# A fused FNet/retention layer with SwiGLU on one core: the seven products of each gate and up set in four parts by token group, in a new order

## The chip, the cores and the metric

The kernel runs on one core of one Trainium2 chip. The metric is device time in microseconds (us), from runs of the whole program; the profile is of one execution of the same program. TensorE is the matmul engine, VectorE, ScalarE and GpSimd work on rows in on-chip memory, and SyncE issues most transfers. In the profile they are PE, DVE, ACT, POOL and SP; PEld is TensorE's load of its stationary operand.

## The reference, cut to what matters

The layer mixes tokens (Fourier and retention heads), normalises, and then runs a SwiGLU on 2048 tokens of width 1024 with 2816 hidden columns. The change lies in the SwiGLU and in the norms just ahead of it:

```python
def swiglu(u, wg, wu, wd):
    return (jax.nn.silu(u @ wg) * (u @ wu)) @ wd
...
        x = layer_norm(DEEPNORM_ALPHA * x + gt1 * mix, ln1_g[l], ln1_b[l])
        u2 = modulate(layer_norm(x), sh2, sc2)
        x = layer_norm(DEEPNORM_ALPHA * x + gt2 * swiglu(u2, w_ffn_gate[l], w_ffn_up[l], w_ffn_down[l]),
                       ln2_g[l], ln2_b[l])
```

All inputs are f32. The kernel keeps f32 accuracy with f16 operands by splitting each number into a high and a low half.

## The kernel before, in words

**Products.** `u2 @ wg` and `u2 @ wu` are computed as 2x2 block products in the form of Strassen and Winograd: seven products in place of eight. Their names are A11, A12, A22 (blocks of the tokens' matrix) and S1 to S4 (sums and differences of such blocks, made by `left`). `right` makes the seven weight operands of one set, with subtracts on GpSimd and a split of each into halves (`split`: high half on ScalarE, L148, low half on VectorE, L149). One product is four steps over k of three matmuls each (`mm3`: high by high, high by low, low by high; L152 to L154), so twelve matmuls of 128x128 by 128x512.

**Sets.** The hidden columns are cut into 11 tiles (`j`), each with a gate set and an up set; a set is seven products for each of two token groups (`sb` 0 and 1). The operands of group 0 are the tiles u2b0 to u2b6 (read back from DRAM; in the order, the digit is the product: 0 A11, 1 A12, 2 S2, 3 S3, 4 A22, 5 S1, 6 S4), those of group 1 are u2a0 to u2a6 (written in place by the last norms).

**Banks.** Products that share a sum accumulate onto one PSUM bank. Bank x (proj for group 0, misc for group 1) takes A11, then S2, S3 and A22; between them ScalarE copies what stands in it (L1323): p after A11, a after S2, b after S3. The next product on x waits for the copy. Bank z (s0 and s1, in the profile both "s") takes S1, from which the fourth quadrant is b + z, and then S4, from which the second is a + z. Bank tq or zt takes A12. VectorE does the sums (L1310 for gate, L1317 for up), ScalarE the silu (L1311, L1308). `keep` copies, `done` sums, `product` ties both to a product. The first gate set is different: five of its products for group 0 run ahead of the last norms' transposes (`late()`), each in a bank of its own, and `alone` takes them up later.

**What sets the order.** Each engine runs its instructions in the order of the program, which a scheduler has interleaved by their dependencies and the order of the code. ORDER gives the seven products' sequence, and `right` makes the operands in that sequence. Weight operands live in a ring of 12 tiles (`ws_tile`, eight taken per set), raw weights in a ring of three (`raw_tile`). `down(i, c)` prepares the down weights beside the sets and stores them in DRAM; `down_last()` does this for the last tile, ahead of the last gate set. `u2_part` transposes and modulates the normalised rows xh (L1060) into q (L1071 to L1078), makes the seven operands and splits them (low halves in L1085).

Of the kernel before, what the change touches and what calls it, by code (L numbers as in the profile page):

```python
# [9 lines left out]
F32 = mybir.dt.float32  # L10
F16 = mybir.dt.float16
AF = mybir.ActivationFunctionType
ALU = mybir.AluOpType
PSUM = bass.MemoryType.PSUM

P = 128
# [63 lines left out]
def layer_kernel(ctx: ExitStack, tc: tile.TileContext, a, out):  # L80
# [50 lines left out]
    def ws_tile(shape=(P, 2, 512), dt=F16):  # L131
        return mk(wp, list(shape), dt, tag="ws", bufs=12)
# [828 lines left out]
    ORDER = (A11, A12, S2, S1, S3, A22, S4)  # L961
# [10 lines left out]
    def right(qa, qb):  # L972

        q0, q1, q2, q3 = qa[:, 0], qa[:, 1], qb[:, 0], qb[:, 1]
        ops = []

        def op(src):
            w = ws_tile()
            split(w[:, 0], w[:, 1], src)
            ops.append(w)  # L980

        t1 = ws_tile((P, 512), F32)
        op(q0)
        op(q2)
        G.tensor_tensor(q0, q1, q0, ALU.subtract)
        G.tensor_tensor(t1, q3, q0, ALU.subtract)
        G.tensor_tensor(q1, q3, q1, ALU.subtract)
        G.tensor_tensor(q2, q2, t1, ALU.subtract)

        for src in (t1, q0, q1, q2, q3):  # L990
            op(src)
        return [ops[ORDER.index(o)] for o in range(7)]

# [30 lines left out]
    def out_proj(t, between=None, last=False):  # L1024
# [12 lines left out]
        if last:  # L1037

            es_z.close()
            ub = es_l.enter_context(tc.tile_pool(name="u2b", bufs=1, reuse_waits="tile"))  # L1040
            for o in range(2, 7):
                u2_early(o, ub)
# [20 lines left out]
    def u2_part(sb, i, xh):  # L1063
# [18 lines left out]
        for o, src in enumerate(ops):  # L1082
            dst = u2[1][o][:, i] if sb else us[:, o]
            S.copy(dst[:, :, 0], src)
            (V if o in (2, 5) or (sb and i == 3 and o != 4) else G).tensor_tensor(dst[:, :, 1], src, dst[:, :, 0], ALU.subtract)  # L1085
# [23 lines left out]
    FIRST = 5  # L1109
    TAGS = ("proj", "misc", "proj", "misc", "s0")  # L1110
    TLAST = ("tq", "zt", "s1")
    late = None
    for sb in (0, 1):
        for i in range(4):
            if sb and i == 1:
                es_u.close()
                ue = es_l.enter_context(tc.tile_pool(name="u2e", bufs=1, reuse_waits="tile"))
                u2_early(0, ue)
                u2_early(1, ue)
# [16 lines left out]
    first = {(o, 0): prod(w0, o, 0, (TAGS[o],)) for o in range(FIRST)}  # L1136
    late()
    es_b.close()
# [111 lines left out]
    for j in range(HJ):  # L1250
# [37 lines left out]
        if j == HJ - 1:  # L1288
            down_last()
        for gu, src in enumerate((wg_in, wu_in)):  # L1290
# [8 lines left out]
            else:  # L1299
                w = w_ops(w_raws(src, j))  # L1300
            st = [{}, {}]
# [31 lines left out]
            def alone(o, sb, ps):  # L1333

                d = st[sb]
                if o == A11:
                    keep(sb, "p", ps)
                elif o == A12:
                    done(sb, 0, d["p"], ps)
                elif o == S2:  # L1340
                    d["a"] = mk(cq, [P, 512], tag="a", bufs=2)
                    V.tensor_tensor(d["a"], d["p"], ps, ALU.add)
                elif o == S3:
                    d["b"] = mk(cq, [P, 512], tag="b", bufs=2)
                    V.tensor_tensor(d["b"], d["a"], ps, ALU.add)
                elif o == A22:
                    done(sb, 2, d["b"], ps)
                elif o == S1:
                    V.tensor_tensor(d["a"], d["a"], ps, ALU.add)
                    done(sb, 3, d["b"], ps)  # L1350
                else:
                    done(sb, 1, d["a"], ps)

# [23 lines left out]
            if j == 0 and gu == 0:  # L1377
                for o in range(7):
                    alone(o, 0, first[o, 0] if (o, 0) in first else prod(w, o, 0, ALL_BANKS))
# [14 lines left out]
            else:  # L1394
                for o in ORDER:
                    for sb in range(2):
                        product(o, sb)
# [274 lines left out]
```

## Time and profile before

| | |
|---|---|
| median of 3 runs | 2142.61 us (2142.06 to 2146.86) |
| profiled execution | 2139.36 us |
| its span | 2137.5 us |
| mean granted clock of TensorE | 0.981 |
| busy: TensorE | 2029.4 us (95%) |
| busy: VectorE | 1404.2 us (66%) |
| busy: ScalarE | 792.0 us (37%) |
| busy: GpSimd | 764.3 us (36%) |

The span goes from the first to the last instruction of the profiled execution; 1.86 us of its time lie around it. The gate and up sets run from about 904 to 1750 us. "Busy" of TensorE counts a matmul until its modelled end. In rows of a timeline the numbers are the start and the duration in us; what stands in brackets is the idle time before the instruction and the instruction (engine, tile, line) that ended it.

### The profile page before, as it was taken

The numbers are of one execution on the slowest core, as the hardware profiler recorded it, in microseconds if no ns is written. First come the engines' busy times: TensorE is split into PE (matmuls) and PEld (weight loads), VectorE is DVE, ScalarE is ACT, GpSimd is POOL, SyncE is SP. The second block draws the span as 40 slices with busy tenths as digits, with TensorE's granted clock in tenths as the row PEclk, the third lists the DMA queues.
The fourth block names the chain that finished last, engine by engine and source line by source line (L and its number), as shares of the span: only waits on it lengthen the run. The fifth ranks groups of instructions, "written<-read, shape, count | busy, mean of one in ns | idle before, by whom it ended". The sixth has DMA issues, their size and how long they took to land. (4 is left out here: it accounts for less than half of the span.)

```text
span 2137.5 us, 30994 instructions
## 1 busy us (share of the span) xinstructions
PE 2029.4 (95%) x11678; PEld 1180.2 (55%) x11678; DVE 1404.2 (66%) x2545; ACT 792.0 (37%) x1436; POOL 764.3 (36%) x804
## 2 busy tenths in 40 slices
PE   6899989999999899979999999999999889999998
PEld 4456576468558444434444444444444348888743
DVE  7976384766547577786566556656664557878776
ACT  5625432242233244443433343334333324333132
POOL 3323312221222156556575557556755300000010
PEclk8999999999999999989999999999999999999999
DMA  9631122331311555634544444444444269665652
GB/s 289 189 107 55 33 64 69 115 95 50 92 37 60 168 169 200 231 119 123 161 126 134 126 144 125 140 122 142 131 144 150 71 224 333 215 220 205 244 183 104
DMA packets 300342, 305.19 MB, mean 143 GB/s; under 512 B 15448, under 2 KB 248992, under 8 KB 299040
## 3 DMA queue, kind: packets, MB, share of 16 engines
q1 hardware_dynamic: 293376, 287.08, 42.1%
q10 hardware_dynamic: 6816, 16.12, 2.0%
q8 instruction: 92, 1.51, 0.3%
q14 instruction: 58, 0.48, 0.1%
HBM read 200.25 MB, written 102.90 MB: 142 GB/s over the span
## 5 line engine op out<-in xcount | busy, mean ns | idle before, releaser
L152 PE MATMUL proj<-ws,uhi 128*128 128x512 f16 (+1 forms) x768 | 251.1, 327 | 4.4 <-ACT sg L774 3.2
L154 PE MATMUL proj<-ws,ulo 128*128 128x512 f16 (+1 forms) x768 | 251.2, 327 | 0.0
L153 PE MATMUL proj<-ws,uhi 128*128 128x512 f16 (+1 forms) x768 | 251.0, 327 | 0.0
L153 PEld LDWEIGHTS <-ws 128*128 128x128 f16 x1296 | 128.0, 99 | 173.2 <-issue 22.5
L152 PEld LDWEIGHTS <-ws 128*128 128x128 f16 x1296 | 127.9, 99 | 155.9 <-issue 7.6
L154 PEld LDWEIGHTS <-ws 128*128 128x128 f16 x1296 | 127.6, 98 | 155.4 <-issue 5.9
L167 POOL TENSOR_TENSOR rstd<-ve,mhalf 128x1 f32<-128x1 f32 x66 | 38.2, 589 | 451.3 <-DVE ve L165 438.1
L149 DVE SCALAR_TENSOR_TENSOR ws<-raw,ws 128x512 f16<-128x512 f32 x186 | 147.9, 810 | 63.4 <-ACT ws L148 62.3
L148 ACT ACTIVATE ws<-raw 128x512 f16<-128x512 f32 x186 | 112.5, 624 | 96.9 <-DMA raw<-in_w_ffn_gate_dram 25.3
L1157 ACT CAST ho<-h 128x1280 f16<-128x1280 f32 x70 | 87.4, 1258 | 148.4 <-DVE h L1429 37.2
L152 PE MATMUL proj<-u2b,ws 128*128 128x512 f16 x344 | 129.6, 381 | 10.8 <-ACT b L1323 8.7
L152 PE MATMUL misc<-u2a,ws 128*128 128x512 f16 x344 | 131.1, 381 | 4.7 <-ACT b L1323 3.9
L149 DVE SCALAR_TENSOR_TENSOR wdo<-raw,wdo 128x256 f16<-128x256 f32 (+1 forms) x100 | 67.6, 700 | 101.5 <-ACT wdo L148 99.6
L153 PE MATMUL proj<-u2b,ws 128*128 128x512 f16 x344 | 131.1, 381 | 0.0
L154 PE MATMUL misc<-u2a,ws 128*128 128x512 f16 x344 | 131.1, 381 | 0.0
L153 PE MATMUL misc<-u2a,ws 128*128 128x512 f16 x344 | 130.9, 381 | 0.0
L154 PE MATMUL proj<-u2b,ws 128*128 128x512 f16 x344 | 130.8, 381 | 0.0
L1158 DVE TENSOR_TENSOR ho<-h,ho 128x1280 f16<-128x1280 f32 x70 | 103.8, 1486 | 21.4 <-ACT ho L1157 21.3
L153 PEld LDWEIGHTS <-uhi 128*128 128x128 f16 x768 | 75.6, 98 | 47.1 <-issue 5.5
L154 PEld LDWEIGHTS <-ulo 128*128 128x128 f16 x768 | 75.6, 98 | 44.8
L152 PEld LDWEIGHTS <-uhi 128*128 128x128 f16 x768 | 76.0, 99 | 42.9 <-issue 1.3
L149 DVE SCALAR_TENSOR_TENSOR wdo<-ws,wdo 128x512 f16<-128x512 f32 (+2 forms) x70 | 53.7, 788 | 69.3 <-ACT wdo L148 66.9
(494 smaller groups left out, 5310.2 us busy)
## 6 DMA issues: line engine op xcount, KB each, us to landing
h<-h SPq DMA_DIRECT2D x40, 640.0 KB
raw<-in_w_mod_dram SPq DMA_DIRECT2D x88, 256.0 KB
wd<-wdo SPq DMA_DIRECT2D x50, 448.0 KB
wd<-wd SPq DMA_DIRECT2D x33, 640.0 KB
h<-sg SPq DMA_DIRECT2D x60, 256.0 KB
raw<-in_w_ffn_gate_dram SPq DMA_DIRECT2D x22, 512.0 KB
raw<-in_w_ffn_up_dram SPq DMA_DIRECT2D x22, 512.0 KB
raw<-in_w_ffn_down_dram SPq DMA_DIRECT2D x40, 256.0 KB
```

The lines of the kernel that those rows point to most:

```text
L148: S.activation(hi, raw, AF.Copy, scale=scale)
L149: V.scalar_tensor_tensor(lo, raw, scale, hi, ALU.mult, ALU.subtract)
L152: T.matmul(o, sh, mh, start=first, stop=False, skip_group_check=onto)
L153: T.matmul(o, sh, ml, start=False, stop=False, skip_group_check=onto)
L154: T.matmul(o, sl, mh, start=False, stop=last, skip_group_check=onto)
L167: pows.append(G.tensor_tensor(rstd, ve, mhalf[:, 0:n], ALU.pow).ins)
L1157: S.copy(dst[:, 0], src)
L1158: V.tensor_tensor(dst[:, 1], src, dst[:, 0], ALU.subtract)
```

## The change

The new order of the products is A11, S1, S2, A12, S3, A22, S4, and the weight operands are made in it. In the gate and up sets the seven go in four parts, (A11, S1), (S2), (A12, S3), (A22, S4), and each part runs first for group 0, then for group 1. In the first gate set all seven products of group 0 run ahead of the last transposes, onto shared banks with kept copies, and their sums are made there (`plus`, `first_products`). In the second last pair of token tiles four low halves move from GpSimd to VectorE. `down_last()` is called after the last up set's weight operands instead of ahead of the last gate set. The number of matmuls is the same.

```diff
     A11, A12, S2, S3, A22, S1, S4 = range(7)
-    ORDER = (A11, A12, S2, S1, S3, A22, S4)
+    ORDER = (A11, S1, S2, A12, S3, A22, S4)
...
         t1 = ws_tile((P, 512), F32)
+
         op(q0)
+        G.tensor_tensor(q0, q1, q0, ALU.subtract)
+        op(q0)
+        G.tensor_tensor(t1, q3, q0, ALU.subtract)
+        op(t1)
         op(q2)
-        G.tensor_tensor(q0, q1, q0, ALU.subtract)
-        G.tensor_tensor(t1, q3, q0, ALU.subtract)
         G.tensor_tensor(q1, q3, q1, ALU.subtract)
+        op(q1)
         G.tensor_tensor(q2, q2, t1, ALU.subtract)
-
-        for src in (t1, q0, q1, q2, q3):
-            op(src)
+        op(q2)
+        op(q3)
...
-            (V if o in (2, 5) or (sb and i == 3 and o != 4) else G).tensor_tensor(dst[:, :, 1], src, dst[:, :, 0], ALU.subtract)
+            (V if o in (2, 5) or (sb and i >= 2 and o != 4) else G).tensor_tensor(dst[:, :, 1], src, dst[:, :, 0], ALU.subtract)
...
     w0 = w_ops(raws0)
-    first = {(o, 0): prod(w0, o, 0, (TAGS[o],)) for o in range(FIRST)}
+    first = {}
+
+    def plus(dst, t, ps):
+        V.tensor_tensor(dst, t, ps, ALU.add)
+        return dst
+
+    def first_products():
+
+
+        def kept(ps):
+            t = ws_tile((P, 512), F32)
+            S.copy(t, ps)
+            return t
+
+        x = prod(w0, A11, 0, ("proj",))
+        p = kept(x)
+        z = prod(w0, S1, 0, ("misc",))
+        prod(w0, S2, 0, None, x)
+        a_ = kept(x)
+        y = prod(w0, A12, 0, ("misc",))
+        prod(w0, S3, 0, None, x)
+        b_ = kept(x)
+        first[3] = plus(ws_tile((P, 512), F32), b_, z)
+        v = prod(w0, A22, 0, ("s0",))
+        prod(w0, S4, 0, None, z)
+        return (0, p, y), (2, b_, v), (1, a_, z)
+
+    sums0 = first_products()
     late()
+    for quad, t, ps in sums0:
+        first[quad] = plus(t, t, ps)
...
-        if j == HJ - 1:
-            down_last()
...
                 w = w_ops(w_raws(src, j))
+                if j == HJ - 1 and gu:
+                    down_last()
...
             if j == 0 and gu == 0:
-                for o in range(7):
-                    alone(o, 0, first[o, 0] if (o, 0) in first else prod(w, o, 0, ALL_BANKS))
+                for quad, t in first.items():
+                    S.activation(sg[0][:, quad], t, AF.Silu, scale=ISU)
...
-                for o in ORDER:
+
+                for part in (ORDER[0:2], ORDER[2:3], ORDER[3:5], ORDER[5:7]):
                     for sb in range(2):
-                        product(o, sb)
+                        for o in part:
+                            product(o, sb)
```

Three places show how instructions move. The first is TensorE at the last norms of the stage ahead of the first tile, before: the rows are the first matmul of a product (on u2b, by ws) or a transpose of xh; xh_1850 and xh_1872 are the two last token tiles.

```order
L152 MATMUL misc_1884_9470<-u2b3_9317,ws_1878_9422 128x512
...
L152 MATMUL s0_1885_9483<-u2b4_9319,ws_1879_9425 128x512
...
L1071 MATMUL zt_1889_9511<-ident_66,xh_1850_9250 128x128
L1071 MATMUL s1_1887_9497<-ident_66,xh_1872_9402 128x128
...
L152 MATMUL tq_2001_9796<-u2b1_8725,ws_1991_9744 128x512
```

The same place in the changed program:

```order
L152 MATMUL misc_1885_9473<-u2b1_9317,ws_1877_9417 128x512
...
L1074 MATMUL tq_1892_9542<-ident_66,xh_1850_9250 128x128
...
L152 MATMUL proj_1881_9431<-u2b3_9319,ws_1878_9421 128x512
...
L152 MATMUL s0_1888_9502<-u2b4_9321,ws_1879_9425 128x512
...
L152 MATMUL misc_1883_9446<-u2b6_9323,ws_1880_9428 128x512
...
L1074 MATMUL zt_1890_9528<-ident_66,xh_1872_9402 128x128
...
L152 MATMUL proj_1995_9763<-u2b0_8723,ws_1988_9738 128x512
```

Before, A22 (u2b4) is the fifth and last gate product ahead of the transposes of xh_1872, and the next product is the up set's A12. In the changed program S3, A22 and S4 stand between the transposes of xh_1850 and those of xh_1872, which makes seven, and the up set's A11 follows.

The second place is ScalarE between the copies a (of the last but one tile's up set) and b, before: ws_2708 to ws_2714 are the last gate set's weights, ws_2730 and ws_2731 the last up set's.

```order
L1323 COPY a_2663_15184<-misc_2656_15109 128x512
L148 ACTIVATE ws_2709_15475<-raw_2706_15469 128x512
L148 ACTIVATE ws_2710_15482<-ws_2707_15471 128x512
L148 ACTIVATE ws_2711_15485<-raw_2705_15467 128x512
L148 ACTIVATE ws_2712_15488<-raw_2705_15467 128x512
L148 ACTIVATE ws_2713_15491<-raw_2706_15469 128x512
L148 ACTIVATE ws_2714_15494<-raw_2706_15469 128x512
L148 ACTIVATE ws_2730_15702<-raw_2727_15697 128x512
L1323 COPY b_2666_15224<-proj_2654_15094 128x512
L148 ACTIVATE ws_2731_15705<-raw_2728_15699 128x512
L1323 COPY b_2668_15242<-misc_2656_15109 128x512
```

The same place in the changed program, where ws_2718 and ws_2719 are the last up set's weights:

```order
L148 ACTIVATE ws_2702_15450<-raw_2694_15425 128x512
L1353 COPY a_2658_15159<-proj_2652_15091 128x512
L1353 COPY a_2659_15173<-misc_2655_15119 128x512
L148 ACTIVATE ws_2718_15658<-raw_2715_15653 128x512
L1353 COPY b_2662_15204<-proj_2652_15091 128x512
L148 ACTIVATE ws_2719_15662<-raw_2715_15653 128x512
L1353 COPY b_2666_15239<-misc_2655_15119 128x512
```

Before, seven splits stand between the copies a and the first b; now one does, and the last gate set's weights (up to ws_2702) stand ahead of the copies a.

The third place is VectorE at the end of a gate set in the middle of the stage, before: sg<-a,s0 and sg<-a,s1 read bank z of the two groups after S4, and ws tiles are the next gate set's weights.

```order
L149 SCALAR_TENSOR_TENSOR wdo_2327_12460<-raw_2314_12381,wdo_2327_12460 128x2x256
L1310 TENSOR_TENSOR sg_2255_11872<-a_2273_11976,s0_2275_11992 128x512
L149 SCALAR_TENSOR_TENSOR ws_2334_12474<-raw_2331_12468,ws_2334_12474 128x512
L1310 TENSOR_TENSOR sg_2256_11873<-a_2274_11990,s1_2276_12005 128x512
L149 SCALAR_TENSOR_TENSOR ws_2335_12481<-ws_2332_12470,ws_2335_12481 128x512
```

The same place in the changed program:

```order
L1340 TENSOR_TENSOR sg_2253_11869<-a_2271_11969,s0_2267_11916 128x512
L149 SCALAR_TENSOR_TENSOR ws_2331_12468<-raw_2328_12463,ws_2331_12468 128x512
L149 SCALAR_TENSOR_TENSOR wdo_2323_12445<-raw_2312_12378,wdo_2323_12445 128x2x128
L149 SCALAR_TENSOR_TENSOR wdo_2323_12445<-ws_2322_12440,wdo_2323_12445 128x4x128
L149 SCALAR_TENSOR_TENSOR wdo_2323_12445<-raw_2312_12378,wdo_2323_12445 128x128
L149 SCALAR_TENSOR_TENSOR ws_2332_12472<-raw_2328_12463,ws_2332_12472 128x512
L149 SCALAR_TENSOR_TENSOR wdo_2324_12453<-raw_2311_12373,wdo_2324_12453 128x2x256
L1340 TENSOR_TENSOR sg_2254_11870<-a_2272_11983,s1_2270_11944 128x512
L149 SCALAR_TENSOR_TENSOR wdo_2325_12457<-raw_2312_12378,wdo_2325_12457 128x2x256
```

Before, the split between the two reads takes the second half of the next raw weights (raw_2331). In the changed program the two splits of weights between them take the first half (raw_2328), with four splits of down weights beside them.

## Rows read from the trace of the kernel before

**Rows 1.** Windows: stretch, its us, busy of each engine, PEclk, DMA share, GB/s.

```profile
900.00:950.00 50.00, 34.94 (x152) 17.02 (x151) 42.38 (x66) 25.48 (x44) 20.71 (x17) 0.83 0.42 137
1100.00:1200.00 100.00, 100.00 (x465) 45.37 (x464) 57.02 (x75) 40.53 (x81) 62.17 (x68) 1.00 0.47 140
1600.00:1700.00 100.00, 91.77 (x417) 40.99 (x415) 50.17 (x67) 36.05 (x69) 51.36 (x48) 0.98 0.40 125
1700.00:1800.00 100.00, 92.00 (x617) 60.87 (x616) 58.01 (x64) 32.91 (x42) 5.21 (x4) 0.98 0.70 258
```

**Rows 2.** Waits of TensorE, whole span: total us, times, longest.

```profile
PE s L1071 <- ACT xh L1060: 16.0, 6, 9.7
...
PE s L152 <- DVE c L1317: 2.4, 1, 2.4
```

**Rows 3.** Timeline of TensorE at the last norms.

```profile
907.73 0.55 PE L1071 MATMUL s<-ident,xh 128*128 128x128 f32 x3 [1.38 <-ACT xh L1060]
...
909.10 0.38 PE L154 MATMUL proj<-u2b,ws 128*128 128x512 f16 x1
...
929.82 0.69 PE L1071 MATMUL s<-ident,xh 128*128 128x128 f32 x2 [9.66 <-ACT xh L1060]
...
934.32 0.63 PE L152 MATMUL tq<-u2b,ws 128*128 128x512 f16 x1
...
938.92 0.38 PE L152 MATMUL zt<-u2a,ws 128*128 128x512 f16 x1
941.91 0.61 PE L153 MATMUL zt<-u2a,ws 128*128 128x512 f16 x1 [2.61 <-DVE u2a L1085]
...
945.90 0.38 PE L152 MATMUL s<-u2a,ws 128*128 128x512 f16 x1
...
948.49 0.38 PE L152 MATMUL proj<-u2b,ws 128*128 128x512 f16 x1
```

**Rows 4.** Timelines of VectorE, GpSimd and ScalarE beside it.

```profile
918.89 3.21 DVE L1085 TENSOR_TENSOR u2a<-sums,u2a 128x512 f16<-128x512 f32 x2
922.01 3.19 DVE L1054 TENSOR_TENSOR r<-r,ln_g 128x512 f32<-128x512 f32 x2
...
937.93 1.76 DVE L1085 TENSOR_TENSOR u2a<-q,u2a 128x512 f16<-128x512 f32 x1
...
941.17 0.68 DVE L1085 TENSOR_TENSOR u2a<-q,u2a 128x512 f16<-128x512 f32 x1
...
917.01 4.53 POOL L1085 TENSOR_TENSOR u2a<-q,u2a 128x512 f16<-128x512 f32 x3
...
928.96 1.52 ACT L1060 ACTIVATE xh<-r,nmr,rstd 128x512 f32<-128x512 f32 x2 [7.58 <-DVE nmr L169]
```

**Rows 5.** Waits of TensorE from 990 to 1062 us, the first tiles.

```profile
PE proj L152 <- ACT b L1323: 2.3, 2, 1.5
PE proj L152 <- ACT p L1323: 2.1, 2, 1.3
PE misc L152 <- ACT b L1323: 2.0, 1, 2.0
PE misc L152 <- ACT p L1323: 0.9, 1, 0.9
```

**Rows 6.** Timelines of TensorE and ScalarE at the passage to the last tile.

```profile
1620.74 0.38 PE L152 MATMUL proj<-u2b,ws 128*128 128x512 f16 x1 [1.95 <-ACT b L1323]
...
1661.34 0.38 PE L152 MATMUL proj<-u2b,ws 128*128 128x512 f16 x1 [4.40 <-ACT b L1323]
...
1667.66 0.38 PE L152 MATMUL misc<-u2a,ws 128*128 128x512 f16 x1 [1.88 <-ACT b L1323]
...
1654.52 0.63 ACT L148 ACTIVATE ws<-raw 128x512 f16<-128x512 f32 x1 [5.30 <-DMA raw<-in_w_ffn_gate_dram]
...
1660.73 0.56 ACT L1323 COPY b<-proj 128x512 f32<-128x512 f32 x1
```

**Rows 7.** Timelines at the end of a gate set: last matmul of S4, then VectorE's read of its bank.

```profile
1266.17 0.38 PE L154 MATMUL s<-u2a,ws 128*128 128x512 f16 x1
...
1273.46 0.67 DVE L1310 TENSOR_TENSOR sg<-a,s 128x512 f32<-128x512 f32 x1
```

More of the change, by code (lines that the diff above doesn't have):

```diff
@@ L1040, in out_proj @@
             ub = es_l.enter_context(tc.tile_pool(name="u2b", bufs=1, reuse_waits="tile"))
-            for o in range(2, 7):
+            for o in ORDER[2:]:
                 u2_early(o, ub)
@@ L1106, in w_ops @@
         return [t.rearrange("p s (k n) -> p s k n", k=4) for t in right(*raws)]
-    FIRST = 5
-    TAGS = ("proj", "misc", "proj", "misc", "s0")
     TLAST = ("tq", "zt", "s1")
@@ L1117, in layer_kernel @@
                 ue = es_l.enter_context(tc.tile_pool(name="u2e", bufs=1, reuse_waits="tile"))
-                u2_early(0, ue)
-                u2_early(1, ue)
+                u2_early(ORDER[0], ue)
+                u2_early(ORDER[1], ue)
             if sb and i == 3:
@@ L1331, in done @@
                         plain(*args)
[L1333 to L1352, printed above, removed]
             def product(o, sb, loose=False):
```

## The prediction

> **What bounds the kernel now.** I read the windows first. TensorE decides: in the middle of the feed-forward stage it is busy for 100.00 of 100 us at full clock [rows 1], and the same holds for every window between 1100 and 1600 us. No order of products can win anything there; it can only lose. Time is to be had where TensorE stands still: between 900 and 950 us it is busy for 34.94 of 50 us at a mean clock of 0.83, and from 1600 to 1800 us it lacks 8.23 and 8.00 us [rows 1]. Then the waits of TensorE by what ended them: 16.0 us for the normalised rows xh, 2.6 us for the low halves of u2a, 2.4 us for c at the passage to the down stage [rows 2]. Last the timeline at those places, and the other engines beside it. "Released" below means that the profile names that instruction as the last one waited for.
>
> One product is twelve matmuls; in the warm row from 945.90 to 948.49 us it takes 2.59 us, and the product that starts at 934.32 us takes 4.60 us until 938.92, so that one ran at 1.2 GHz instead of 2.4 and lost 2.0 us [rows 3].
>
> **The last norms (gate of the first tile).** Before, TensorE has five gate products to do, then waits 9.66 us for xh, transposes, makes one up product, and at 941.91 us, one matmul into the next, is held 2.61 us by a low half on VectorE [rows 3]. The xh that is waited for ends one path: VectorE subtracts two low halves of the tile before, multiplies and adds the gains of the last one and takes its moments, and ScalarE makes xh from 928.96 us on [rows 4]. The change puts all seven gate products ahead of the last transposes. The two that are added (S1 and S4) were to be done later anyway, so 2 x 2.59 = 5.2 us of work move into the idle time. They fit: from 907.73 us on, 90 matmuls of 0.216 us (19.4 us) and 28 transposes (the first twelve took 1.4 us, from 907.73 to 909.10 [rows 3]; so 3.2 us) are 22.6 us, and the release lies over 30 us away. In that order TensorE still waits, by my walk through the rows, about 2.3 us for the first xh (six matmuls instead of eleven stand ahead of it, so 1.38 grows by 5 x 0.216), 2 us for the xh of the other token tile (its transposes stand one product earlier), 2.5 us in front of S4, which adds onto the bank that VectorE has to read first, and 3.2 us at the end; all lie inside the 30 us.
>
> The end of the stage is the next term. Before, the second matmul on u2a waits for u2a1, whose subtract runs from 941.17 to 941.85 us. Now the first matmul that takes a low half needs that of u2a0. Its subtract began at 937.93 us and took 1.76 us, while GpSimd subtracted weights beside it; without that neighbour the same form takes 0.68 us [rows 4]. The new code has those GpSimd instructions earlier, so I set 938.6 us, 3.2 us ahead of 941.85. Sum: 5.2 + 3.2 = 8.4 us.
>
> What could move that release is VectorE's queue in front of the last xh. Added are four low-half subtracts taken from GpSimd and one sum of a kept product, 5 x 0.68 = 3.4 us. Removed is GpSimd's company: beside its subtracts from 917.01 us on (three in 4.53 us, two more behind them) two VectorE subtracts take 3.21 us and two multiplies 3.19 us, where 0.68 each is 1.4 us a pair [rows 4]; 1.8 + 1.8 = 3.6 us come back if the slowing is due to that. One subtract stays on GpSimd. I set the two equal. From both sides: 3.4 us later if the slowing has another cause (gain 5.0), 3.6 us of clock besides if the cold stretches at 934.32 and 941.91 us (2.0 and 3.99 - 11 x 0.216 = 1.6 us [rows 3]) go. Bounds 3 to 12.5 us.
>
> **The order of the steady products.** Before, the seven products run in pairs over the token groups; S3 and A22 use one bank (x), and of each pair only one other product stands between S3 and the A22 that must wait for the copy b of the bank. Now two do. In the first tiles this copy cost 2.3 + 2.0 us of waiting and the copy p 2.1 + 0.9 us [rows 5]. The b waits, at most 4.3 us, should go, since the copy gets 2.59 us more and no single wait there is over 2.0; the p waits need not: A11 to S2 is as far apart in time as before for each group. Against that, the other bank (z) comes under less slack: from S4 to the next set's S1 there were seven products of the same kind, now there are three, 7.8 us. I set 3 us for this stage (0 at worst without the z rival below, 7.3 at best). In the steady part I set nothing: 100.00 cannot grow, and the ring of weight tiles is one and a half sets long, so that S1's operand, now needed second instead of fourth, can be made while the set before runs.
>
> **The tenth and the last tile.** TensorE waits 1.95, 4.40 and 1.88 us for b [rows 6]. Behind the 4.40 stand ScalarE's own queue: a split waits 5.30 us for the gate weights, then six more splits are in front of the copy at 1660.73 [rows 6]. These are the last tile's gate weights, loaded behind the whole preparation of the last down weights. That preparation moves behind the up weights, so its two loads and its five products' stores on SP, and its GpSimd subtracts, no longer stand ahead of the gate weights; and b gets 2.59 us of slack. The waits sum to 8.23 us. The product behind the 4.40 wait runs cold too: from 1661.34 to 1665.78 (1667.66 - 1.88) it takes 4.44 us, 1.85 too long [rows 6]. So at most 10.1 us; I take 8. What is late next are the seven splits of the last down weights, which now stand on ScalarE ahead of the copies b of the last gate set; each costs 0.6 us, but some wait for stores to free their tiles. If one such wait of 5.30 us (the nearest row) fell in front of b, less the 2.59 us of new slack, twice, 5.4 us are lost again: 2.6 at worst.
>
> **The passage to down.** The first down product's bank s waited 2.43 us for VectorE's c [rows 2]. In the new program the first down products go to other banks (zt and proj), so that c is read beside them. I take 2.4, with -2 (a copy of ScalarE behind a cast that waits for a transfer) to 4.
>
> **Sum.** 8.4 + 3 + 8 + 2.4 = 21.8 us. The profiled execution took 2139.36 us, of which 2137.5 are its span; 2139.4 - 21.8 = 2117.6. The median of the runs shown, 2142.61, is 3.25 above that execution, so 2120.8 is the forecast. The four terms together reach from 3 + 0 + 2.6 - 2 = 4 to 12.5 + 7.3 + 10.1 + 4 = 34 us; as they do not go wrong together, I give the forecast's own range as 14 to 28, 2114 to 2129.
>
> **Rivals.** *The z bank becomes a wait (slower).* VectorE adds S4's bank to a, and S1 of the next set may not start before. The last matmul of S4 starts at 1266.17 us and ends at 1266.55, and this sum runs from 1273.46 to 1274.13: 7.6 us, against 7.8 us that are left [rows 7]. If VectorE's queue stays as it is and anything comes 0.2 us later, each gate set waits; one product (2.59 us) in each of ten gate sets is 26 us, 2147 us. It decides from 7.8 us on. Against it: the sum was late because the split that stands ahead of it waits for the second half of the next gate weights; in the new order of VectorE only splits of the first half stand there. I give it 0.11.
>
> *The norms give nothing.* S4's wait or VectorE's longer queue push the last xh back, or the clock eats it: three waits of 2 to 3 us in front of four products could leave each of these at 1.2 GHz, 4 x 2.0 = 8 us. In the trace a wait of 1.38 us left the clock at 2.4 GHz (twelve transposes in 1.4 us), waits of 2.61, 4.40 and 9.66 us had matmuls 0.42 us apart behind them [rows 3, 6]. The Trainium skill (TensorE: Matmul & The Clock Gate, section "What's actually happening") holds that the slow clock is the resting state, which activity lifts; the trace agrees, and by that rule this rival is the one to fear. Then 2120.8 + 8.4 = 2129. Chance 0.20.
>
> *Only the stall at the last tile goes*, and the small ones come back as others: 8 us less, some of it given back to the down splits, 2137 to 2142, no change that can be measured. Chance 0.09. That the seven products are not all placed ahead of the last transposes is excluded by the order of the new program.
>
> *Everything goes and the clock stays up*: 28 to 34 us, 2111. Chance 0.06.
>
> **How the numbers follow.** The forecast has 0.54, the rivals 0.11, 0.20, 0.09, 0.06. Faster by over 0.3% (6.4 us, about what a measurement of this kernel can tell from no change) holds the forecast, the norms rival and the last: 0.80; within it 0.09; slower 0.11. From 2110 to 2138 us leaves out the slow rival and half of the no-change case, some 0.16.
>
> **What would show it.** In the new profile: no wait over 4 us on xh between 905 and 945 us, and the first matmul on a low half of u2a near 938.5 us, with eight products done before it; no wait for b above 1 us after 990; the window 1600 to 1700 above 97 us busy; 1100 to 1600 still at 100. Wrong it is if TensorE waits at S1 for VectorE's sums (lines of the new profile with bank s), or if the last xh comes after 931 us.

## The result, and the profile after

The changed kernel takes 2123.01 us (median of 4 runs, 2121.23 to 2124.54) against 2143.3 us of the kernel before (median of 4, 2142.06 to 2146.86): 20.3 us less, ratio 0.9902, 95% interval 0.9885 to 0.992. The profiled execution has a span of 2119.4 us at a mean clock of 0.986.

The windows of the changed kernel, with the columns of [rows 1]:

```profile
900.00:950.00 50.00, 42.86 (x211) 20.74 (x210) 42.26 (x74) 30.99 (x55) 19.92 (x17) 1.00 0.42 137
1000.00:1050.00 50.00, 43.66 (x194) 19.23 (x193) 30.14 (x36) 22.07 (x45) 36.25 (x39) 0.97 0.48 142
1100.00:1200.00 100.00, 100.00 (x465) 45.33 (x463) 57.68 (x77) 42.33 (x85) 57.96 (x62) 1.00 0.45 132
1500.00:1600.00 100.00, 98.47 (x455) 44.35 (x454) 66.09 (x80) 35.04 (x68) 60.96 (x57) 1.00 0.43 136
1600.00:1700.00 100.00, 100.00 (x465) 45.29 (x463) 53.61 (x68) 39.87 (x74) 52.21 (x48) 1.00 0.38 118
1700.00:1800.00 100.00, 94.67 (x719) 69.83 (x717) 71.56 (x77) 36.21 (x44) 4.96 (x4) 1.00 0.82 302
```

Against [rows 1], TensorE is busier at the last norms (42.86 for 34.94 of 50 us), with the clock at 1.00 instead of 0.83, and at the last tile (100.00 for 91.77). Two windows are worse: from 1500 to 1600 us 1.5 us are lost where TensorE was full before, and from 1000 to 1050 us 6.3 us, where the kernel before lost 1.7 at the same clock of 0.97:

```profile
1000.00:1050.00 50.00, 48.35 (x216) 21.43 (x215) 29.90 (x38) 18.68 (x39) 37.87 (x40) 0.97 0.42 128
```

The waits of TensorE in the changed kernel, as in [rows 2]:

```profile
PE s L1074 <- ACT xh L1063: 8.1, 5, 2.4
...
PE misc L152 <- ACT p L1353: 4.7, 5, 3.3
...
PE proj L152 <- ACT a L1353: 4.0, 3, 2.1
...
PE proj L152 <- ACT ws L1148: 3.3, 2, 2.4
...
PE s L152 <- DVE c L1347: 1.9, 2, 1.2
...
PE misc L152 <- ACT u2a L1087: 1.6, 1, 1.6
PE s L152 <- DVE sg L1340: 1.3, 1, 1.3
```

The one wait of 9.66 us for xh is gone, and so are the waits for b of [rows 5] and [rows 6], down to one of 0.3 us. In their place stand waits for the copies p and a.

To see where the time went I compare the traces by stages. Each has the same number of matmul records, 11,678, of the same products, so the time from one record number to another is the time of the same amount of work. The stages end at records 5260 (the last norms, which begin at 5090), 6050 (first tiles, up to 1140 us before), 8250 (middle, up to 1615 us), 8500 (passage to the last tile) and 9050 (last tile and passage to down). Ahead of record 5090, where these programs do the same work, executions differ by -3.2 to +2.8 us from the one before, and behind record 9050 by -1.4 to +0.5; both are left out. The table gives the difference to the kernel before in us (its own stages in the first row); the last column sums the five stages. Each row is one profiled execution. Two programs were profiled twice: the rows of the changed kernel and e10 differ by up to 2.2 us in a stage, those of e6 and e11 by 0.1.

| run | norms | first tiles | middle | tenth to last tile | to down | sum |
|---|---|---|---|---|---|---|
| before, its time | 54.60 | 180.41 | 474.83 | 64.35 | 103.25 | |
| predicted | -8.4 | -3 | 0 | -8 | -2.4 | -21.8 |
| changed | -12.64 | +3.44 | +3.00 | -10.40 | -3.96 | -20.56 |
| changed, again (e10) | -11.13 | +3.09 | +0.76 | -10.40 | -2.98 | -20.66 |
| e1, down preparation back | -11.14 | +2.35 | +1.08 | -0.74 | -1.99 | -10.44 |
| e2, that move alone | -0.12 | -0.15 | 0.00 | -10.40 | 0.00 | -10.67 |
| e3, five first products | +2.80 | -3.44 | +2.96 | -10.40 | -4.04 | -12.12 |
| e5, low halves back | -7.31 | +2.75 | +2.53 | -10.39 | -2.82 | -15.24 |
| e4, pairs | -11.12 | +3.71 | +0.17 | -10.40 | -2.88 | -20.52 |
| e6, other sequence | -11.14 | +0.69 | 0.00 | -10.40 | -2.91 | -23.76 |
| e11, the same again | -11.12 | +0.64 | 0.00 | -10.40 | -3.00 | -23.88 |
| e7, two ht tiles | -11.12 | +2.24 | +7.63 | -10.40 | -3.66 | -15.31 |
| e8, e6 and e7 | -11.13 | +1.54 | +0.11 | -10.40 | -2.75 | -22.63 |
| e9, e6 and sums on VectorE | -11.12 | +0.89 | 0.00 | -10.40 | -2.53 | -23.16 |
| e12, e6 without the first down piece | -11.15 | -9.91 | +19.28 | -10.40 | -1.54 | -13.72 |

The timeline of TensorE at the last norms, changed kernel (compare [rows 3]):

```profile
909.84 0.55 PE L1074 MATMUL s<-ident,xh 128*128 128x128 f32 x3 [1.95 <-ACT xh L1063]
...
917.43 0.38 PE L152 MATMUL proj<-u2b,ws 128*128 128x512 f16 x1 [2.40 <-ACT ws L1148]
...
924.03 0.38 PE L152 MATMUL proj<-u2b,ws 128*128 128x512 f16 x1 [0.93 <-ACT ws L1148]
...
929.53 0.38 PE L152 MATMUL misc<-u2b,ws 128*128 128x512 f16 x1 [0.16 <-DVE ws L1140]
...
932.12 0.38 PE L1074 MATMUL zt<-ident,xh 128*128 128x128 f32 x2
...
933.10 0.38 PE L152 MATMUL proj<-u2b,ws 128*128 128x512 f16 x1
...
935.69 0.60 PE L1074 MATMUL zt<-ident,xh 128*128 128x128 f32 x4
937.91 0.59 PE L152 MATMUL misc<-u2a,ws 128*128 128x512 f16 x2 [1.61 <-ACT u2a L1087]
```

Five waits of 2.4 us at most take the place of one of 9.66, the transposes of the last xh follow the seventh product at once, and the up product from 933.10 to 935.69 takes 2.59 us, where the one of [rows 3] took 4.60.

This execution is not the usual one. In the repeat of the same kernel (e10) the first xh comes later against TensorE (it ends 4.22 us after record 5090, here 2.71), and so it does in the eight other runs with these instructions; the low half that ends the stage comes as much later, 33.26 us after the record for 31.75, and this is the 1.5 us between the first profile's norms stage and the others'. The timeline of TensorE in e10:

```profile
908.18 0.90 PE L1074 MATMUL s<-ident,xh 128*128 128x128 f32 x3 [3.46 <-ACT xh L1063]
...
910.79 0.63 PE L153 MATMUL proj<-u2b,ws 128*128 128x512 f16 x1
...
922.37 0.38 PE L152 MATMUL proj<-u2b,ws 128*128 128x512 f16 x1 [0.52 <-ACT ws L1148]
```

The twelve transposes behind the wait of 3.46 us take 2.61 us there and not 1.4, and the matmuls behind them start 0.43 us apart until 914.21: that is 1.2 GHz. It delays nothing, since TensorE waits less afterwards (0.52 us where the first profile has 2.40 and 0.93).

### The profile page after: what moved, and what is told of

Read it like the earlier page. It is cut to its first block, busy times and chain, and to the rows that moved or that the text cites. A ratio compares the mean times of both kernels' runs of the same rounds, so it can differ in the third digit from the quotient of the medians.

```text
span 2119.4 us, 30963 instructions
## 1 busy us (share of the span) xinstructions
PE 2025.6 (96%) x11678; PEld 1178.6 (56%) x11678; DVE 1408.6 (66%) x2546; ACT 795.0 (38%) x1438; POOL 757.0 (36%) x800
## 4 chain that ended last, share of the span: by engine, by line
PE 57%; DVE 17%; DMA 9%; POOL 8%; ACT 4%; issue 3%; SPq 2%; POOLq 0%; DVEq 0%; ACTq 0%
PE proj L152 8%; PE proj L154 8%; PE proj L153 8%; PE misc L152 4%; PE misc L154 4%; PE misc L153 4%; PE s L152 3%; PE s L154 3%; PE s L153 3%; DMA raw<-in_w_mod_dram 3%; DVE raw L377 2%; DVE ws L149 2%; DMA raw<-in_w_ffn_down_dram 1%; DVE st L178 1%; POOL us L1088 1%
## 5 line engine op out<-in xcount | busy, mean ns | idle before, releaser
L1188 DVE TENSOR_TENSOR ho<-h,ho 128x1280 f16<-128x1280 f32 x70 | 103.9, 1489 | 20.2 <-ACT ho L1187 20.1
L149 DVE SCALAR_TENSOR_TENSOR wdo<-ws,wdo 128x512 f16<-128x512 f32 (+2 forms) x70 | 58.7, 861 | 50.4 <-ACT wdo L148 49.4
```

Of the source, the lines that this page charges most:

```text
L149: V.scalar_tensor_tensor(lo, raw, scale, hi, ALU.mult, ALU.subtract)
L1188: V.tensor_tensor(dst[:, 1], src, dst[:, 0], ALU.subtract)
```

## The experiments

**What won the time between the tenth and the last tile.** e1 puts the preparation of the last down weights back, e2 does this move alone in the kernel before.

```diff
 e1 (on the changed kernel; e2 is the reverse, on the kernel before)
+        if j == HJ - 1:
+            down_last()
         for gu, src in enumerate((wg_in, wu_in)):
...
-                if j == HJ - 1 and gu:
-                    down_last()
```

> The changed kernel with the preparation of the last down weights put back ahead of the last gate set. If its move carries the 10.4 us that were won between 1610 and 1670 us, the wait for the copy b of 4 us or so comes back there and the time is 8 to 10 us above the changed kernel, about 2132. Rival: the won time is due to the order of the parts, which gives the copy b one product (2.59 us) more; then at most 4.40 - 2.59 = 1.8 us of wait come back, 2123 to 2125.

> The kernel before with only that move. If the move carries it, the three waits of 1.95, 4.40 and 1.88 us and the slow product behind go: 8 to 10 us below the kernel before, about 2134. Rival (the order of the parts carries it): no change, 2143. Both needed: in between, 2138 to 2140.

e1 took 2130.11 us (ratio to the kernel before 0.9956, 0.9941 to 0.9972), e2 2124.52 (0.9941, 0.9921 to 0.9962). By stages, e2 has the whole 10.40 us and e1 keeps 0.74 of it. The move carries it alone; the slack of b gives nothing measurable beside it. The timeline of TensorE in e1 says why:

```profile
1608.84 0.38 PE L152 MATMUL proj<-u2b,ws 128*128 128x512 f16 x1 [1.79 <-ACT b L1353]
...
1643.14 0.58 PE L152 MATMUL proj<-u2b,ws 128*128 128x512 f16 x1 [5.16 <-ACT a L1353]
```

With the new order the late splits stand in front of the copy a instead of b, and TensorE waits 5.16 us for that one. A queue that is held up does not care which copy stands behind the held instruction.

**What won the time at the norms.** e3 goes back to five products, each in its own bank; e5 puts four low halves back on GpSimd.

```diff
 e3
-    sums0 = first_products()
+    first = {(o, 0): prod(w0, o, 0, (TAGS[o],)) for o in range(FIRST)}
     late()
...
 e5
-            (V if o in (2, 5) or (sb and i >= 2 and o != 4) else G).tensor_tensor(dst[:, :, 1], src, dst[:, :, 0], ALU.subtract)
+            (V if o in (2, 5) or (sb and i == 3 and o != 4) else G).tensor_tensor(dst[:, :, 1], src, dst[:, :, 0], ALU.subtract)
```

> The changed kernel with five instead of seven gate products ahead of the last transposes, each in a bank of its own as before; order, parts, low halves and down preparation as changed. If the two added products and the clock that stays up are the gain of the norms (12.65 us), a wait of 8 to 10 us for xh and matmuls 0.43 us apart come back, and the time is 9 to 13 us above the changed kernel, 2132 to 2136. Rival: the gain comes from the low halves on VectorE, then the time is within 3 us of the changed kernel.

> The changed kernel with the four low halves put back on GpSimd. If VectorE's queue and GpSimd's company weigh the same, as the prediction set them, xh comes within 1 us and the time is that of the changed kernel, 2122 to 2125. Rival (the four subtracts on VectorE push xh back, as its start at 930.70 instead of 928.96 us may be read): xh starts near 929 us again and 1 to 2 us are won. Second rival (GpSimd's company costs more): 3 us or more lost.

e3 took 2123.82 us (0.993, 0.9908 to 0.9951), not the 2132 to 2136 expected: at the norms it is 2.80 us slower than the kernel before, 13.9 to 15.4 us above the changed one, but in the first tiles 6.5 to 6.9 us below it. Its timeline of TensorE:

```profile
907.53 0.90 PE L1074 MATMUL s<-ident,xh 128*128 128x128 f32 x3 [3.46 <-ACT xh L1063]
...
928.19 0.69 PE L1074 MATMUL s<-ident,xh 128*128 128x128 f32 x2 [3.14 <-ACT xh L1063]
...
935.03 0.59 PE L152 MATMUL zt<-u2a,ws 128*128 128x512 f16 x1 [2.13 <-ACT u2a L1087]
...
940.42 0.61 PE L153 MATMUL zt<-u2a,ws 128*128 128x512 f16 x1 [4.81 <-DVE u2a L1088]
```

The single long wait became several, and the mean clock from 900 to 950 us is 0.76. The low half that ends the stage comes no earlier than before (37.11 us after record 5090, before 37.17). So the low halves on VectorE win nothing by themselves; with seven products they do: e5 took 2124.54 us (0.9937, 0.9917 to 0.9957) and its norms stage wins 7.31 us instead of 11.1 to 12.6. Two things are in that. Beside GpSimd's five subtracts the pairs on VectorE slow down as in [rows 4]. And the scheduler put S4 behind the last transposes; the timeline of TensorE in e5:

```profile
921.02 0.38 PE L152 MATMUL proj<-u2b,ws 128*128 128x512 f16 x1 [1.44 <-ACT ws L1148]
...
929.53 0.44 PE L1074 MATMUL zt<-ident,xh 128*128 128x128 f32 x2 [3.17 <-ACT xh L1063]
...
930.59 0.63 PE L152 MATMUL misc<-u2b,ws 128*128 128x512 f16 x1
...
934.52 0.27 PE L1074 MATMUL zt<-ident,xh 128*128 128x128 f32 x1
```

TensorE waits 3.17 us for xh, and S4 behind it takes 3.93 us (930.59 to 934.52) at 1.2 GHz for most of it. In the changed kernel S4 fills that wait. The trace parts the two: in e5 the first xh ends 2.78 us after record 5090, as in the first profile of the changed kernel (2.71), so those two can be compared. Between them e5 loses 5.3 us (7.31 for 12.64). The last xh ends 1.55 us later (26.70 for 25.15 us after the record), behind the slow pairs in VectorE's queue; from there to the low half of u2a0 pass 10.38 us and not 6.60, with S4 in between, which is the other 3.8 us.

**What the four parts cost.** e4 runs the new order in pairs over the groups, e6 in another sequence.

```diff
 e4
-                for part in (ORDER[0:2], ORDER[2:3], ORDER[3:5], ORDER[5:7]):
-                    for sb in range(2):
-                        for o in part:
-                            product(o, sb)
+                for o in ORDER:
+                    for sb in range(2):
+                        product(o, sb)
 e6
+                for o, sb in ((A11, 0), (A11, 1), (S1, 0), (S2, 0), (S1, 1), (S2, 1), (A12, 0), (S3, 0), (A12, 1), (S3, 1), (A22, 0), (S4, 0), (A22, 1), (S4, 1)):
+                    product(o, sb)
```

> The changed kernel with the products of a set in pairs over the two token groups, in the new order. If the parts make the new waits for the copies p and a (6.4 us lost between 950 and 1610 us), these go and the b waits of the kernel before (4.3 us in the first tiles) come back: 2119 to 2124. Rival: the waits come from the new order of the weight operands on ScalarE; then they stay and the b waits come on top: 2126 to 2130.

> The changed kernel with another sequence in a set: A11/0 A11/1 S1/0 S2/0 S1/1 S2/1 A12/0 S3/0 A12/1 S3/1 A22/0 S4/0 A22/1 S4/1 (number = group). Between a copy and the product that needs it there are three products instead of two for p of group 1 and for a of group 0, two instead of three for p of group 0. If two products are too few for a copy behind ScalarE's casts, the 4.7 us on p of group 1 and most of the 4.0 us on a go, and 3 to 6 us are won: 2117 to 2120. Rival: the copies come as late as ScalarE's queue lets them, and the wait moves to p of group 0: 2122 to 2126.

e4 took 2119.02 us (0.9903, 0.9883 to 0.9923) and e6 2115.86 (0.989, 0.9871 to 0.991). The middle is where the parts cost: +3.00 and +0.76 us in the two executions of the changed kernel, +0.17 in e4, 0.00 in e6. In the first profile the waits there are 0.2 to 0.7 us each, for p of group 1 and a of group 0. These two copies have two products between them and the next product on their bank; with three, in e4 and in e6, the waits are gone. The number alone does not decide: p of group 0 in e6 has two as well, every b in the changed kernel has two and before and in e4 one, and none of these makes a wait of 0.2 us in the middle.

In the first tiles e4, without the parts, has +3.71. The waits for p and a are gone there too, as the theory had it, but not the loss. TensorE waits for other instructions instead, on bank s above all (waits of e4 from 900 to 1800 us; of the 5.6 us for c, 4.27 stand at 1000.68 us, the rest at the passage to down):

```profile
PE s L152 <- DVE c L1347: 5.6, 2, 4.3
PE s L152 <- DVE sg L1340: 3.6, 2, 1.9
...
PE proj L152 <- ACT b L1353: 2.7, 1, 2.7
```

e6 has +0.69 there, and its largest wait is 3.51 us for p of group 0, as the rival had it.

**Two theories for the first tiles that fell.** e7 takes two tiles for the split sums (ht), e8 both e6 and e7, e9 takes e6 and puts the first tile's sums on VectorE.

```diff
 e7, e8
-                ht = mk(cq, [P, 2, 512], F16, tag="ht", bufs=1)
+                ht = mk(cq, [P, 2, 512], F16, tag="ht", bufs=2)
...
-                    c = mk(cq, [P, 512], tag="c", bufs=2)
+                    c = mk(cq, [P, 512], tag="c", bufs=1)
 e9
-                eng = V if j == HJ - 1 and sb else G
+                eng = V if j == 0 or (j == HJ - 1 and sb) else G
...
-                (V if j == HJ - 1 and sb else G).tensor_tensor(s4, h[1], sums[sb][:, 1], ALU.subtract)
+                (V if j == 0 or (j == HJ - 1 and sb) else G).tensor_tensor(s4, h[1], sums[sb][:, 1], ALU.subtract)
```

> The changed kernel with two tiles instead of one for the split sums that go to DRAM (ht), and one instead of two for c (only VectorE writes and reads c). If the waits for p and a come from ScalarE's casts into ht, which wait for the transfer out of the one tile and stand ahead of the copies, they go: 3 to 6 us won, 2117 to 2120. Rival (number of products between): no change, 2123.

> The sequence of the run before the last with the two ht tiles of the last. If both causes are one (a copy late by the cast's wait), it wins no more than the better of the two, 2117 to 2119; if they are two, 2114 to 2117, and the middle of the stage is back at 100.00 of 100 us everywhere from 1100 to 1700 us.

> The kernel with the sequence A11/0 A11/1 S1/0 S2/0 S1/1 S2/1 A12/0 S3/0 A12/1 S3/1 A22/0 S4/0 A22/1 S4/1, and the sums of the first tile's products that go to the down stage on VectorE instead of GpSimd (eight instructions). In the changed kernel GpSimd is busy for 17.34 of 20 us from 990 to 1010 us, a split on ScalarE waits 4.93 us for its subtract, and the copies p behind the split hold TensorE for 0.9 and 3.3 us. If GpSimd's queue gives back there what the norms won, the waits for p in the first tiles go and the stretch after the norms takes 3 to 6 us less than in the run with this sequence alone: 2110 to 2113 where that one stands at 2116. Rival: VectorE is as full (16.70 of 20 us), the waits move to the splits' low halves and sums: the same within 1 us, or slower.

e7 took 2123.4 us (0.9923, 0.9902 to 0.9944): 0.9 to 1.2 us less in the first tiles, where the wait of 3.3 us for p stays, and 4.6 to 6.9 us more in the middle, where TensorE waits six times for a, 4.6 us in all. What makes these waits the run does not show; it also takes a tile from c. e8 took 2116.71 (0.9899, 0.9876 to 0.9922), no better than e6. The casts into ht are not what holds p. e9 took 2115.78 us (0.9887, 0.9872 to 0.9902), +0.89 in the first tiles where e6 has +0.69: GpSimd's sums are not it either; the wait for p is 3.58 us there, behind splits that still wait for other engines.

**The cause in the first tiles.** In these traces GpSimd stood still ahead of the waits, for a load. The first row is GpSimd, the others are SyncE's: five stores of the first piece of the down weights (merged into one row), a sixth, and the load; changed kernel:

```profile
983.06 1.26 POOL L987 TENSOR_TENSOR ws<-raw,raw 128x512 f32<-128x512 f32 x1 [10.91 <-DMA raw<-in_w_ffn_gate_dram]
...
957.04 19.35 SPq L1221 DMA_DIRECT2D wd<-wdo  x5
977.07 0.37 SPq L1210 DMA_DIRECT2D wd<-wdo  x1
977.55 0.65 SPq L1104 DMA_DIRECT2D raw<-in_w_ffn_gate_dram  x1
```

The same in the kernel before:

```profile
987.28 1.27 POOL L987 TENSOR_TENSOR raw<-raw,raw 128x512 f32<-128x512 f32 x1 [10.49 <-DMA raw<-in_w_ffn_gate_dram]
...
981.72 0.82 SPq L1101 DMA_DIRECT2D raw<-in_w_ffn_gate_dram  x1
```

The second load of the second tile's gate weights is issued 4.2 us earlier than before, while TensorE is over 10 us further on. Raw weights have three buffers, and the load waits until the first piece of the down weights leaves one: VectorE's last low half out of it ends at 977.05 us. SyncE's queue holds it as well, with the six stores ahead, which wait 20.2 us in all for low halves of that piece. GpSimd's idle time alone proves nothing: for the same load of later tiles it stands still for 9.59 and 8.93 us (until 1271.72 and 1343.81 us, kernel before), and TensorE loses nothing there. e12 moves the piece to the sixth tile:

```diff
 e12 (on e6)
-        if j < 2 * HP:
+        if 0 < j < 2 * HP:
             down(j // 2, j % 2)
+        if j == 5:
+            down(0, 0)
```

> The kernel with the sequence that puts A11 of both groups first, and the preparation of the first piece of the down weights moved from the first tile to the sixth, where two pieces stand in one tile. In all runs so far GpSimd waits 10.5 to 11 us, until about 983 us, for the second load of the second tile's gate weights, which SyncE issues at 977 to 982 us only, since its buffer held down weights; what the norms win reaches that load with 4 of 10 us. If this chain gives the gain back in the first tiles, the load is issued 15 us or more earlier, the waits for p, c and sg up to 1060 us go (5 to 7 us), and the stretch from 956 us on takes 3 to 6 us less than before the change, instead of 0.7 more: 2108 to 2111 where the sequence alone had 2113. The price: two pieces in the sixth tile, 0 to 5 us there, seen in the middle stage. Rival: copies and sums are late by their own engines' queues, and the stretch stays within 1 us.

SyncE issues that load in e12 at 948.23 us:

```profile
948.23 0.60 SPq L1104 DMA_DIRECT2D raw<-in_w_ffn_gate_dram  x1
```

TensorE then has no wait at all between 945 and 1065 us, and the first tiles take 9.91 us less than before the change, 10.6 less than in e6. So the first piece of the down weights is what holds the first tiles, with about twice the size I had put. That it does so by the load is the likely way and not shown: e12 takes the buffer's hold away together with the stores ahead of the load and with the piece's own work (GpSimd is busy for 30.71 of 60 us from 945 us on and not 41.05 as in e6, VectorE for 36.78 and not 41.94, ScalarE for 22.11 and not 26.07). A run that frees only the buffer, with a fourth one, would part them. The price is larger than expected too: 19.28 us in the middle, where the sixth and the seventh tile take 82.0 and 82.3 us and not 72.5, and e12 took 2123.89 us (0.9929, 0.9915 to 0.9942). Three of the waits of TensorE there:

```profile
1328.75 0.38 PE L152 MATMUL proj<-u2b,ws 128*128 128x512 f16 x1 [4.25 <-ACT p L1353]
...
1351.02 0.38 PE L152 MATMUL proj<-u2b,ws 128*128 128x512 f16 x1 [2.51 <-ACT b L1353]
...
1372.78 0.38 PE L152 MATMUL proj<-u2b,ws 128*128 128x512 f16 x1 [3.47 <-ACT p L1353]
```

**The changed kernel and the better sequence side by side.** Two runs on one chip:

> The changed kernel as it is, beside the runs it is compared with: 0.990 of the kernel before, and by stages as in its first profile: 12.6 us less at the last norms, 3.4 and 3.0 more up to the tenth tile, 10.4 less there and 4.0 less at the passage to down. The rival is that the first stage's number was one execution's: 11.1 us, as the other runs with the same instructions there had.

> The sequence of the best run again, beside the changed kernel on one chip. If the two-product distances cost the changed kernel 5 to 6 us (3.0 us in the middle, 2 to 3 in the first tiles), this one is 4 to 6 us below it. Rival: the difference between the two came from different sets of runs: within 2 us.

The changed kernel took 2121.07 us (0.9914, 0.99 to 0.9928), e6's sequence 2113.24 (0.9879, 0.9866 to 0.9893), 2140.36 the kernel before. The intervals do not overlap. The gap of 7.8 us is above the 4 to 6 expected; by stages it is 0.76 us in the middle and 2.45 in the first tiles, 3.2 us. The two profiled executions are 4.1 us apart, and what the other runs lose besides no trace shows. This sequence beats both kernels. The rival on the norms stage also held: 11.1 us there is what nine of the ten runs with those instructions show, and the 12.64 of the first profile is one execution's.

## Why the prediction was right, and where it was not

The time came out 2.2 us above the forecast and the gain at 20.3 us of 21.8, inside the range, but the terms were off in both directions: against the first profile the norms won 4.2 us more than forecast, the last tile 2.4 and the passage to down 1.6, and the first tiles were 6.4 and the middle 3.0 us worse. That the total came out so close is in part luck.

*The last norms: right in mechanism, too small.* 8.4 us were forecast, 11.1 to 12.6 came. VectorE's subtract for u2a0 in the changed kernel ends at 938.83 us:

```profile
938.14 0.69 DVE L1088 TENSOR_TENSOR u2a<-q,u2a 128x512 f16<-128x512 f32 x1
```

Eight products stood before it, as forecast. This execution was 2.4 us behind the one before when the stage began, so the release came 941.85 - (938.83 - 2.39) = 5.4 us earlier and not 3.2; in e10 and the eight like it it came 3.9 us earlier. The waits of the walk were not those that came: 1.95 us for the first xh (2.3 in the walk), none for the xh of the other token tile (2), 0.16 in front of S4 (2.5) and 1.61 at the end (3.2). The two others, 2.40 and 0.93 us, are for the kept copies of bank x, which the walk left out. All of it lies ahead of the release, so it changed nothing in the sum. Missing was the clock: I had kept the cold stretches of [rows 3] in the sum, and only as a bound let them go. The one behind the release (1.6 us) went, and two matmuls on high halves (0.4 us) now run ahead of it: 5.2 + 5.4 + 1.6 + 0.4 = 12.6 us in the first profile, and 5.2 + 3.9 + 1.6 + 0.4 = 11.1 in the others. The rival that feared the clock was right about the clock and wrong about the time: in the first profile none of the waits left a product at 1.2 GHz; in the nine others matmuls ran at it behind the wait for the first xh (3.46 us in e10), but ahead of the release, where it cost nothing. The Trainium skill (TensorE: Matmul & The Clock Gate, section "What's actually happening") has the slow clock as the resting state that activity lifts. The trace agrees with it in e10 and e5, where the matmuls behind waits of 3.46 and 3.17 us run slow and speed up while TensorE works.

*The low halves: set at nothing, wrong.* I let 3.4 us more on VectorE and 3.6 us back from GpSimd's company cancel. Against the kernel before that was nearly so: counted from record 5090 the last xh ends 0.65 us earlier in the first profile and 0.85 later in e10. (It ends at 932.22 us, past the 931 that I gave as a sign of being wrong, but in an execution that runs 2.4 us late.) But e5 loses 5.3 us against the first profile, 1.55 by a later xh and the rest by where S4 then falls.

*The first tiles: wrong sign.* The failed step is "the b waits, at most 4.3 us, should go [...] I set 3 us for this stage". The b waits went, down to 0.3 us. One reading in that step was wrong: "A11 to S2 is as far apart in time as before for each group" holds for group 0 (three products between) but not for group 1, which has two now and had three, and the longest wait, 3.28 us, is for p of group 1. But e4 has three there, without waits for p and a, and loses as much, so this reading alone does not account for the loss. What I did not ask is what sets the pace of the copies. In the traces their engine waits for splits, these for GpSimd, this for a load, and that for a buffer that the down weights hold. That chain moved by 4.2 us when TensorE moved by over 10, so part of the gain was waited for again, at p, a, c and sg: 3.1 to 3.4 us lost. e12 shows that it is the down piece that holds them; through which of its links is argued from the traces. e3 fits: TensorE comes 2.80 us later there, and the first tiles win 3.44. That this is near the 3 forecast does not confirm the 3, since a TensorE that comes later waits less whatever the order. The timeline of TensorE in the changed kernel, for [rows 5]:

```profile
975.09 0.38 PE L152 MATMUL s<-u2a,ws 128*128 128x512 f16 x1 [1.29 <-DVE sg L1340]
...
1004.27 0.38 PE L152 MATMUL proj<-u2b,ws 128*128 128x512 f16 x1 [0.94 <-ACT p L1353]
...
1010.31 0.38 PE L152 MATMUL misc<-u2a,ws 128*128 128x512 f16 x1 [3.28 <-ACT p L1353]
...
1017.76 0.38 PE L152 MATMUL proj<-u2b,ws 128*128 128x512 f16 x1 [2.12 <-ACT a L1353]
```

*The middle: set at nothing, 0.8 to 3.0 us lost.* "100.00 cannot grow" held, but it fell: I checked the distances of the banks x (for b) and z, and took p and a as unchanged in time. For a of group 0 and p of group 1 two products stand in between instead of three. e4 and e6 show the loss to be that of the sequence. The z bank, the rival that would have made the kernel slower, made no wait of 0.2 us in the middle. On bank s, which I gave as a sign of being wrong, TensorE waits 1.29 and 0.73 us in the first tiles and 1.21 in the last, far from the 2.59 us per set that the rival had.

*The tenth and the last tile: right, and its second reason idle.* 8 us forecast, 10.40 came, above the 10.1 that I had as a bound from [rows 6]; the stage has every wait and the cold product of those rows. e2 shows that the move does it alone. The feared splits of the last down weights cost nothing there.

*The passage to down: right in sign, by other waits*, 3.0 to 4.0 for 2.4. e2 has 0.00 there and e4 without the parts 2.88, so the new order gives it. But the wait for c that was to go shrank from 2.43 to 1.21 us. A wait of 3.79 us for `state` went, and one of 3.17 for a low half of ho came, and neither was in the prediction. The first two rows are the kernel before, the others the changed one:

```profile
1751.65 0.27 PE L152 MATMUL s<-wd,ho 128*128 128x256 f16 x1 [2.43 <-DVE c L1317]
1764.74 0.37 PE L152 MATMUL s<-wd,ho 128*128 128x256 f16 x1 [3.79 <-ACT state L1488]
...
1730.36 0.38 PE L152 MATMUL s<-u2a,ws 128*128 128x512 f16 x1 [1.21 <-DVE c L1347]
1744.19 0.28 PE L154 MATMUL misc<-ws,ho 128*128 128x256 f16 x1 [3.17 <-DVE ho L1188]
```

So the size of this term is luck.

## What to carry to other kernels

When the engine that bounds the kernel gets ahead at one place, follow each operand that it needs next back to its load and the buffer the load waits for: if that chain does not move as far, part of the gain is given back a few steps later, at a wait that names some innocent copy. When an in-order queue is held by one instruction, move what holds it; giving the copy behind it more slack moves the wait to another copy. Count the products between each copy and the next product on its bank for every kept value, not only for those that waited before, and look at what stands ahead of the copy on its engine: the count alone did not tell which copy was late. Profile a program twice before a stage's number is explained.

## What the runs showed of the hardware that was not expected

TensorE's clock stood at 1.00 from 900 to 950 us in the first profile of the changed kernel, with waits of 1.95, 2.40, 0.93 and 1.61 us in it, at 0.93 in e10, the same kernel, with 3.46, 0.52, 0.15 and 1.62 us, and at 0.76 in e3 with 3.46, 3.14, 2.13 and 4.81 us among its waits.

The length of a wait alone does not tell whether what follows is slow. Behind the wait of 3.28 us for p at 1010.31 us in the changed kernel 24 matmuls start 0.22 us apart; behind the next one, of 2.12 us at 1017.76, the first six start 0.22 us apart and the next eight 0.40 to 0.43. In the kernel before a wait of 1.99 us has slow matmuls behind it:

```profile
999.35 0.38 PE L152 MATMUL misc<-u2a,ws 128*128 128x512 f16 x1 [1.99 <-ACT b L1323]
...
1000.16 0.63 PE L152 MATMUL misc<-u2a,ws 128*128 128x512 f16 x1
```

The matmuls from 1000.16 to 1003.15 us start 0.43 us apart. So a wait of 2 us can have slow matmuls behind it and one of 3.28 none, and the loss can come after TensorE has resumed.
